# First projection of a hybrid decoder layer cut into quarters, with its convolution moved behind the second projection

## The chip, the cores and the metric

The kernel runs on one core of one Trainium2 chip. The metric is the device time of one execution in microseconds (us). Five engines of the core work from queues of their own, each in program order: PE (TensorE, the matmuls), DVE (VectorE), ACT (ScalarE), POOL (GpSimd) and SP (SyncE, which issues most of the transfers). Waits between them are semaphores.

## The reference, cut to what matters

One decoder layer for 256 tokens of width 1024: a mixer with four branches, a layer norm, a mixture of 16 experts, a layer norm. The change touches only the beginning of branch B (gated DeltaNet):

```python
proj = jnp.einsum("bsd,de->bse", x, w_in)          # x: 256 x 1024, w_in: 1024 x 10264
qkv = jax.nn.silu(causal_depthwise_conv(gdn_qkv, gdn_conv_w))   # gdn_qkv: 1536 columns of proj
q, k, v = jnp.split(qkv, [512, 1024], axis=-1)
```

## The kernel before

**Precision.** Every float32 operand of a projection is split in two parts that TensorE multiplies fast: a high part (a cast by ACT) and the rest (a subtraction by DVE, float32 minus high part). A product of two such operands is three matmuls: high by high, high by low, low by high. `split` does this for the transposed input (`xh`, `xl`), `parts` for a piece of weight (`whi`, `wlo`).

**Projections.** `w_in` is taken in pieces of 256 columns (1 MB). `fetch` loads a piece into one of three buffers `raw`, which it takes in turn. `proj_cm` casts a piece in two blocks of 128 columns (`parts`, three buffers each for `whi` and `wlo`) and multiplies each block by the whole of x: 24 matmuls of 256 columns for a block, 48 for a projection, into a PSUM tile `pcm` of pool `pmm`. This pool has three buffers, so the fourth projection waits until all readers of the first projection's tile are done, the fifth until those of the second are, and so on.

**The beginning.** Four transfers on SP bring x in halves (256 KB each), then come the first piece of weight in two halves, the second piece whole, thirteen small transfers (`prm_r`, `hp8`: parameters), and then the third piece and what follows. PE transposes x in groups of four 128x128 blocks (L264); ACT and DVE split each group (L101, L102). A projection's step `b_in(ci)` multiplies and then runs the causal convolution: per block one ACT scaling (L407) and three DVE multiply-adds (L410) that read the projection's PSUM tile. Its taps come from `taps()` (L336 to L340): PE transposes the parameters, DVE copies them out and scales them.

**What sets the order.** The text ORDER lists the steps. Inside that, a scheduler orders the instructions of PE, DVE, ACT and POOL; SP's are left in the order of the code. The steps at the start are `bi.0 cc bi.1 bi.2 cq.0 bi.3`: projections 1, 2 and 3 for branch B with their convolutions (`cc` computes constants in many tiny DVE operations), the fourth projection `cq.0` for branch C, the fifth for B again. All transfers share eight completion semaphores in rotation, and a transfer that takes a semaphore waits at its issue until the transfer eight places before it has landed.

Of the kernel before, what the change touches and what calls it, by code (L numbers as in the profile page):

```python
# [8 lines left out]
F32 = mybir.dt.float32  # L9
# [32 lines left out]
bi.0 cc bi.1 bi.2 cq.0 bi.3 sm bi.4 cq.1 bi.5 bs gg.0 bp.0 ll bv.0 cq.2 bp.1 bo lg.0  # L42
# [10 lines left out]
def trunk(ctx: ExitStack, tc: tile.TileContext, a, out):  # L53
# [45 lines left out]
    def split(ps, hi, lo, scale=None):  # L99
        if scale is None:  # L100
            A.copy(hi, ps)  # L101
            V.tensor_tensor(lo, ps, hi.bitcast(F32), op=OP.subtract)  # L102
# [7 lines left out]
    def fetch(src, cuts=1):  # L110
# [4 lines left out]
        for c in range(cuts):  # L115
            cs = slice(c * n // cuts, (c + 1) * n // cuts)
            Q.dma_start(raw[:, :, cs], src[:, :, cs])
        return raw

    def parts(raw, k0, nk, c0, n, one=None):  # L120
# [6 lines left out]
        cuts = (slice(0, nk),) if one is None else (slice(0, nk // 2), slice(nk // 2, nk))  # L127
        for c in cuts:
            if one is None:
                A.copy(hi, src)  # L130
            else:
                A.activation(hi[:, c], src[:, c], AF.Copy, scale=one)  # L132
        for c in cuts:
            V.tensor_tensor(lo[:, c], src[:, c], hi[:, c].bitcast(F32), op=OP.subtract)  # L134
# [68 lines left out]

    ones = mk.tile([128, 128], F32, name="ones")
    G.memset(ones, 1.0)
    one = cst.tile([128, 1], BF16, name="one")
# [52 lines left out]
    one0 = cst.tile([128, 1], F32, name="one0")  # L259
    for kg in range(2):  # L260
        for n in range(2):
            p = pb("pxt")
            for k in range(4):
                T.transpose(p[:, k, :], x0[n][:, (4 * kg + k) * 128:(4 * kg + k + 1) * 128], ident)  # L264
            split(p, xh[:, 4 * kg:4 * kg + 4, n * 128:(n + 1) * 128],
                  xl[:, 4 * kg:4 * kg + 4, n * 128:(n + 1) * 128])
    A.activation(one0, xh[:, 4, 0:1].bitcast(F32), AF.Copy, scale=0.0, bias=1.0)
# [1187 lines left out]
```

## Time and profile before

| | us |
|---|---|
| runs of the kernel before: median (lowest, highest) | 612.0 (611.89, 613.32) |
| the profiled execution, device time | 614.47 |
| its span, first to last instruction | 612.7 |
| PE busy in the span | 586.7 |
| DVE busy | 323.9 |
| ACT busy | 253.1 |

The profile is one execution. Times in its rows count from the start of the span. A row of the timeline gives start, duration, engine, line, operation, what it writes and reads, shape and count; in brackets stands how long the engine was idle before and what released it. When one instruction had several waits the profile names only one releaser, and it can name the wrong one: the program's order tells which instruction a wait is on.

### The profile page before, as it was taken

To read this page: it belongs to the slowest core of one execution; us is meant where nothing else is said; L and a number is where in the kernel's file an instruction comes from. 1 tells how busy PE (TensorE), PEld (TensorE's weight loads), DVE (VectorE), ACT (ScalarE), POOL (GpSimd) and SP (SyncE) were. 2 spreads that over 40 slices of the span, in tenths; PEclk is the share of its full clock that TensorE was granted. 3 is DMA by queue.
4 is the path that set the end of the run, shared out by engine and by line. 5 is a ranking of instruction groups with operands and counts; after the bars stand their busy time and mean duration, and the time that the engine had idled before them with its cause. 6 is when DMAs were issued, how large, how long until landed. Compare 5 with 4: busy or idle time off the path is not lost. (4 is left out here: it accounts for less than half of the span.)

```text
span 612.7 us, 10555 instructions
## 1 busy us (share of the span) xinstructions
PE 586.7 (96%) x4231; PEld 458.9 (75%) x4231; DVE 323.9 (53%) x651; ACT 253.1 (41%) x413; POOL 20.2 (3%) x53
## 2 busy tenths in 40 slices
PE   6999999999999999999999999999999999999992
PEld 5999999989988999999999999633633634444351
DVE  3799788678458955865656655552210300111245
ACT  5556664473478747644444444311201211021121
POOL 3000010100102000000000000000000000000000
PEclk9999999999999999999999999999999999999996
DMA  7877454632221564398998794789999999999931
GB/s 208 227 226 200 138 153 137 210 107 85 86 70 34 174 208 138 118 329 319 387 357 306 262 406 193 291 333 403 418 415 408 415 416 409 416 416 407 417 160 72
DMA packets 86380, 160.43 MB, mean 262 GB/s; under 512 B 9963, under 2 KB 56161, under 8 KB 86326
## 3 DMA queue, kind: packets, MB, share of 16 engines
q1 hardware_dynamic: 86198, 159.44, 71.6%
q8 instruction: 35, 0.57, 0.4%
q0 software_dynamic: 128, 0.26, 0.2%
q14 instruction: 19, 0.16, 0.1%
HBM read 158.50 MB, written 1.18 MB: 261 GB/s over the span
## 5 line engine op out<-in xcount | busy, mean ns | idle before, releaser
L134 DVE TENSOR_TENSOR wlo<-raw,whi 128x1024 fp32r<-128x1024 f32 (+1 forms) x106 | 126.0, 1200 | 53.7 <-ACT whi L130 53.0
L130 ACT CAST whi<-raw 128x1024 fp32r<-128x1024 f32 x102 | 106.1, 1047 | 97.6 <-DMA raw<-in_w_in_dram 33.0
L272 PE MATMUL pcm<-xh,whi 128*128 128x256 f32 x512 | 125.9, 284 | 1.9 <-ACT whi L132 1.5
L276 PE MATMUL pcm<-xl,whi 128*128 128x256 f32 x512 | 125.0, 282 | 0.0
L272 PEld LDWEIGHTS pcm<-xh,whi 128*128 128x128 f32 x512 | 97.2, 190 | 2.7 <-ACT whi L132 1.9
L276 PEld LDWEIGHTS pcm<-xl,whi 128*128 128x128 f32 x512 | 97.3, 190 | 0.1
L281 PE MATMUL pcm<-xh,wlo 128*128 128x256 f32 x512 | 71.6, 281 | 1.3 <-DVE wlo L134 1.1
L281 PEld LDWEIGHTS pcm<-xh,wlo 128*128 128x128 f32 x512 | 65.4, 189 | 1.7 <-DVE wlo L134 1.7
L102 DVE TENSOR_TENSOR dd<-pd,dd 128x512 fp32r<-128x512 f32 (+1 forms) x18 | 11.4, 632 | 95.3 <-ACT dd L101 95.3
L1303 PE MATMUL pd<-ew,sh 128*64 128x512 f32 (+1 forms) x288 | 56.8, 546 | 0.7 <-ACT sh L1364 0.7
L1292 PE MATMUL wu<-ew,xg 128*64 128x512 f32 x256 | 57.4, 593 | 0.0
L1292 PE MATMUL wg<-ew,xg 128*64 128x512 f32 x256 | 56.7, 595 | 0.6 <-issue 0.6
L1303 PEld LDWEIGHTS pd<-ew,sh 128*64 128x64 f32 x288 | 20.4, 137 | 35.1 <-issue 29.4
L1292 PEld LDWEIGHTS wu<-ew,xg 128*64 128x64 f32 x256 | 18.5, 137 | 36.2 <-issue 34.4
L1292 PEld LDWEIGHTS wg<-ew,xg 128*64 128x64 f32 x256 | 18.1, 137 | 33.5 <-issue 32.1
L272 PE MATMUL ptm<-whi,xh 128*128 128x256 f32 x128 | 32.5, 287 | 0.0
L272 PE MATMUL pbr<-yth,whi 128*128 128x256 f32 x128 | 32.1, 284 | 0.0
L276 PE MATMUL pbr<-ytl,whi 128*128 128x256 f32 x128 | 32.0, 282 | 0.0
L274 PE MATMUL ptm<-whi,xl 128*128 128x256 f32 x128 | 31.5, 281 | 0.0
L101 ACT CAST dd<-pd 128x512 fp32r<-128x512 f32 (+1 forms) x18 | 9.7, 538 | 46.3 <-PE pd L1303 46.3
L1209 ACT ACTIVATE xg<-pxg,gbp 128x128 f32<-128x128 f32 x32 | 13.2, 456 | 36.7 <-DVE xg L1208 35.7
L1343 DVE SCALAR_TENSOR_TENSOR sh<-wu,cw,sh 128x512 f32<-128x512 f32 x8 | 6.0, 750 | 37.9 <-PE wu L1292 37.8
(420 smaller groups left out, 887.4 us busy)
## 6 DMA issues: line engine op xcount, KB each, us to landing
raw<-in_w_in_dram SPq DMA_DIRECT2D x39, 1024.0 KB, 5.3
ew<-in_w_gate_dram SPq DMA_DIRECT2D x64, 512.0 KB, 9.8
ew<-in_w_up_dram SPq DMA_DIRECT2D x64, 512.0 KB, 9.7
ew<-in_w_down_dram SPq DMA_DIRECT2D x64, 512.0 KB, 9.8
raw<-in_w_branch_dram SPq DMA_DIRECT2D x8, 1024.0 KB
raw<-in_w_out_dram SPq DMA_DIRECT2D x4, 1024.0 KB
x<-in_x_dram SPq DMA_DIRECT2D x4, 256.0 KB, 5.3
raw<-in_w_in_dram SPq DMA_DIRECT2D x2, 512.0 KB
```

What stands on the lines that cost most here:

```text
L101: A.copy(hi, ps)
L102: V.tensor_tensor(lo, ps, hi.bitcast(F32), op=OP.subtract)
L130: A.copy(hi, src)
L134: V.tensor_tensor(lo[:, c], src[:, c], hi[:, c].bitcast(F32), op=OP.subtract)
L272: T.matmul(o, sh(k), mh(k), start=first and k == 0, stop=False)
L274: T.matmul(o, sl(k), mh(k), start=False, stop=False)
L276: T.matmul(o, sh(k), ml(k), start=False, stop=False)
L281: T.matmul(o, sl(k), mh(k), start=False, stop=last and k == kt - 1)
L1209: A.activation(xg[1][:, 2 * kg + k, :], ps[kg][:, k, 128:256], AF.Identity, scale=g_, bias=b_)
L1292: P(T.matmul(p[r, :], xg[pr][:, k, r], W[pr, (nm, e, k // 2)][:, k % 2, :], start=k == 0, stop=k == 7))
L1303: P(T.matmul(p[r, :], hT[:, k, r], W[pr, ("wd", e, k)][:, 0, c0:c1], start=k == 0, stop=k == 3))
L1343: V.scalar_tensor_tensor(sg, pu, cw[pr // 2][:, pr % 2:pr % 2 + 1], sg, op0=OP.mult, op1=OP.mult)
```

## The change

- x comes in quarters of 256 columns (eight transfers of 128 KB on SP), and the first piece of weight in four transfers of 256 KB, each with two of its eight row blocks and all 256 columns, issued by ACT instead of SP, one for each quarter of x. The third piece of weight is fetched in the code of the beginning too, behind the small parameters.
- `first_proj` replaces `proj_cm` for the first projection. It goes by quarters: transposes, split and casts of the next quarter stand in front of this quarter's 12 matmuls, and one PSUM accumulation runs over both blocks. In front of it, and between the first two transposes, stand 14 and 8 matmuls on a tile of zeros (`warm`), whose result is not used.
- The weight parts of the second projection are made at the end of `first_proj`. `b_in(0)` stops after its products; `b_in(1)` runs `taps()`, then the first convolution, then its own. In ORDER, `bi.1` stands ahead of `cc`.
- Several instructions are kept in the order of the code (`keep`, `K`). A constant 1.0 that was computed from xh (`one0`) is a memset (`one1`) now.

```diff
-bi.0 cc bi.1 bi.2 cq.0 bi.3 sm bi.4 cq.1 bi.5 bs gg.0 bp.0 ll bv.0 cq.2 bp.1 bo lg.0
+bi.0 bi.1 cc bi.2 cq.0 bi.3 sm bi.4 cq.1 bi.5 bs gg.0 bp.0 ll bv.0 cq.2 bp.1 bo lg.0
...
-    for h in range(2):
+    w0 = w_in[:, :, C_GQ:C_GQ + 256]
+    raw0 = [fetch(w0, 0)]
+    for q in range(4):
+        cs = slice(256 * q, 256 * q + 256)
         for n in range(2):
-            Q.dma_start(x0[n][:, 512 * h:512 * h + 512], xin[:, n, 512 * h:512 * h + 512])
-    raw0 = [fetch(w_in[:, :, C_GQ + 256 * j:C_GQ + 256 * j + 256], 2 - j) for j in range(2)]
+            Q.dma_start(x0[n][:, cs], xin[:, n, cs])
+        A.dma_start(raw0[0][:, 2 * q:2 * q + 2], w0[:, 2 * q:2 * q + 2])
+    raw0.append(fetch(w_in[:, :, C_GQ + 256:C_GQ + 512]))
...
+    raw0.append(fetch(w_in[:, :, C_GQ + 512:C_GQ + 768]))
...
+    def first_proj():
+        p = pmm.tile([128, 2, S], F32, name="pcm", tag="mm")
...
+        warm(14)
+        x_part(0)
+        w_part(0)
+        warm(8)
+        for q in range(4):
+            if q < 3:
+                x_part(q + 1)
+                w_part(q + 1)
+            hi = hl[q // 2][0][:, 2 * (q % 2):2 * (q % 2) + 2]
+            for k in range(2 * q, 2 * q + 2):
+                for b in range(2):
+                    for x in (xh, xl):
+                        K(T.matmul(p[:, b, :], hi[:, k % 2, 128 * b:128 * b + 128], x[:, k, :],
+                                   start=q == 0 and k == 0 and b == 0 and x is xh, stop=False))
+            low(q)
+        v.hl1 = [parts(raw0[1], 0, 8, 128 * b, 128, K) for b in range(2)]
+        return p
...
-        p = proj_cm(C_GQ + 256 * ci, raw0[ci] if ci < 2 else None, one0 if ci == 0 else None)
+        p = first_proj() if ci == 0 else proj_cm(C_GQ + 256 * ci, raw0[ci] if ci < 3 else None,
+                                                  v.hl1 if ci == 1 else None)
         if ci == 0:
+            v.first = p
+            return
+        if ci == 1:
             taps()
+            conv(0, c4, v.first)
+        conv(ci, c4, p)
```

The built programs show where the scheduler puts this. First DVE, around the first convolution. Before, it reads the first projection's tile (`pcm_216`) between the low parts of the third piece of weight (`raw_396`) and the first of the fourth (`raw_467`); the rows begin in its second block, and `splq` are tiny operations of `cc`:

```order
L134 TENSOR_TENSOR wlo_400<-raw_396,whi_399 128x1024
L410 SCALAR_TENSOR_TENSOR gq_215<-pcm_216,cwh_206,gq_215 128x255
L327 TENSOR_SCALAR splq_299<-splq_299 128x4
L134 TENSOR_TENSOR wlo_428<-raw_396,whi_427 128x1024
L410 SCALAR_TENSOR_TENSOR gq_215<-pcm_216,cwh_206,gq_215 128x254
L326 TENSOR_TENSOR splq_299<-splq_299,spls2_298 128x4
L134 TENSOR_TENSOR wlo_471<-raw_467,whi_470 128x1024
L410 SCALAR_TENSOR_TENSOR gq_215<-pcm_216,cwh_206,gq_215 128x253
L327 TENSOR_SCALAR splq_299<-splq_299 128x4
L410 SCALAR_TENSOR_TENSOR gq_215<-pcm_327,cwh_206,gq_215 128x255
```

The last reader of `pcm_216` stands just behind the first low part of the fourth piece, and the taps stand ahead of all these rows. Now, in the same place, with the third piece as `raw_145`, the fourth as `raw_498`, and the tiles of the first and second projection as `pcm_199` and `pcm_318`:

```order
L129 TENSOR_TENSOR wlo_459<-raw_145,whi_458 128x1024
L129 TENSOR_TENSOR wlo_502<-raw_498,whi_501 128x1024
L387 COPY prm_133<-pp_367 128x128
L388 TENSOR_SCALAR cwh_189<-prm_133 128x48
L395 TENSOR_SCALAR hb_190<-prm_133 128x4
L396 TENSOR_SCALAR hb_190<-prm_133 128x4
L398 TENSOR_SCALAR nlam_395<-prm_133 128x4
L466 SCALAR_TENSOR_TENSOR gq_198<-pcm_199,cwh_189,gq_198 128x255
L466 SCALAR_TENSOR_TENSOR gq_198<-pcm_318,cwh_189,gq_198 128x255
```

The taps (`prm`, `cwh`) have moved behind the first low part of the fourth piece, and the first convolution behind them. Six multiply-adds on block 0 of both tiles in turn begin here; DVE then goes on like this:

```order
L368 TENSOR_SCALAR spls_398<-sple_397 128x4
L129 TENSOR_TENSOR wlo_530<-raw_498,whi_529 128x1024
L466 SCALAR_TENSOR_TENSOR gq_198<-pcm_199,cwh_189,gq_198 128x255
L466 SCALAR_TENSOR_TENSOR gq_198<-pcm_318,cwh_189,gq_198 128x255
L466 SCALAR_TENSOR_TENSOR gq_198<-pcm_199,cwh_189,gq_198 128x254
L466 SCALAR_TENSOR_TENSOR gq_198<-pcm_318,cwh_189,gq_198 128x254
L466 SCALAR_TENSOR_TENSOR gq_198<-pcm_199,cwh_189,gq_198 128x253
L466 SCALAR_TENSOR_TENSOR gq_198<-pcm_318,cwh_189,gq_198 128x253
```

So the last reader of the first projection's tile (`pcm_199`, 128x253) has moved behind both low parts of the fourth piece, with five operations on the second projection's tile in front of it. The first instruction of PE's fourth projection waits on this one (and on ACT) in both programs, since it writes the same PSUM buffer; the fifth projection's waits on the last reader of the second projection's tile, the row below.

Then ACT, at the beginning of its queue. Before:

```order
L101 ACT_TABLE_LOAD
L101 CAST xh_174<-pxt_177 128x4x128 [waits PE_49]
L101 CAST xh_174<-pxt_184 128x4x128 [waits PE_49]
L101 CAST xh_174<-pxt_191 128x4x128 [waits PE_49]
L101 CAST xh_174<-pxt_198 128x4x128 [waits PE_49]
L267 ACTIVATE one0_176<-xh_174 128x1 [waits Activation_49]
L132 ACTIVATE whi_217<-raw_109,one0_176 128x512 [waits DMAHW4_49,Activation_49]
```

Now, with the transfers of the first piece of weight in front:

```order
L145 DMA raw_105<-in_w_in_dram 128x2x256 x3
L145 DMA raw_105<-in_w_in_dram 128x2x256 [waits DMAHW0_49]
L103 ACT_TABLE_LOAD
L103 CAST xh_184<-pxt_214 128x512 [waits PE_49]
L296 CAST whi_221<-raw_105 128x512
L103 CAST xh_184<-pxt_233 128x512 [waits PE_49]
L296 CAST whi_221<-raw_105 128x512 [waits DMAHW3_49]
```

The table load has moved behind four transfers, of which the fourth waits until the first has landed (`DMAHW0_49`).

On SP the row behind the eight quarters of x is the second piece of weight, then the thirteen small transfers, then the third and fourth pieces, as before. From the fifth projection on PE's rows are the same in both programs, and soon after the other engines' are too.

## Rows read from the trace of the kernel before

**Rows 1.** The profile's page, its parts 1 and 2: busy time by engine with its share of the span, and PE's busy tenths in 40 equal slices of the span.

```profile
PE 586.7 (96%) x4231; PEld 458.9 (75%) x4231; DVE 323.9 (53%) x651; ACT 253.1 (41%) x413; POOL 20.2 (3%) x53
PE   6999999999999999999999999999999999999992
```

**Rows 2.** Waits of PE in the whole span: line that waited, for whom, us in total, times, longest.

```profile
PE pn L1416 <- DVE nmc L1412: 5.9, 1, 5.9
...
PE p L570 <- DVE ps L565: 1.7, 2, 0.9
...
PE pcm L272 <- DVE splq L327: 0.4, 1, 0.4
```

**Rows 3.** Stretches of the span: start and end, us, busy us and instructions of PE, its weight loads, DVE, ACT and POOL, then the granted TensorE clock, the share of the DMA engines and GB/s.

```profile
10.20:15.26 5.06, 5.06 (x25) 5.06 (x25) 2.80 (x5) 3.18 (x5) 0.00 (x0) 1.00 0.48 151
...
30.00:60.00 30.00, 29.57 (x250) 29.11 (x249) 28.30 (x76) 18.79 (x30) 0.00 (x0) 1.00 0.77 222
```

**Rows 4.** Timeline of PE: the first transposes of x, the first products of projections 1, 3, 4 and 5, and in front of the fifth the last eight products of the fourth.

```profile
3.60 2.11 PE L264 MATMUL pxt<-ident,x 128*128 128x128 f32 x8 [3.60 <-POOL tri L209]
...
10.20 0.58 PE L272 MATMUL pcm<-xh,whi 128*128 128x256 f32 x1 [1.53 <-ACT whi L132]
...
23.85 0.28 PE L272 MATMUL pcm<-xh,whi 128*128 128x256 f32 x1
...
29.50 0.28 PE L272 MATMUL pcm<-xh,whi 128*128 128x256 f32 x1
...
34.22 1.10 PE L281 MATMUL pcm<-xh,wlo 128*128 128x256 f32 x8
35.70 0.36 PE L272 MATMUL pcm<-xh,whi 128*128 128x256 f32 x1 [0.38 <-DVE splq L327]
```

**Rows 5.** Timeline of SP's issues: the first small transfer that stood until the second piece had landed, the issue of the third, fourth and fifth pieces (one row), and the transfer behind them.

```profile
13.97 0.25 SPq L166 DMA_DIRECT2D prm_r<-in_rg_b_x_dram  x1
...
16.16 2.84 SPq L117 DMA_DIRECT2D raw<-in_w_in_dram  x3
19.05 2.75 SPq L380 DMA_DIRECT2D raws<-in_w_in_dram  x1
```

**Rows 6.** Timeline of ACT: its table load and first cast of x, the casts of the second piece, the first convolution's scaling, and the first casts of the third and fourth pieces, which stood until those had landed.

```profile
0.80 1.28 ACT L101 ACT_TABLE_LOAD   x1 [0.80 <-PEq L1443]
4.73 0.58 ACT L101 CAST xh<-pxt 128x512 fp32r<-128x512 f32 x1 [2.65 <-PE pxt L264]
...
13.97 2.00 ACT L130 CAST whi<-raw 128x1024 fp32r<-128x1024 f32 x2 [1.56 <-DMA raw<-in_w_in_dram]
...
19.00 0.47 ACT L407 ACTIVATE gq<-pcm,cwh 128x256 f32<-128x256 f32 x1 [0.97 <-DVE cwh L340]
...
21.68 1.05 ACT L130 CAST whi<-raw 128x1024 fp32r<-128x1024 f32 x1 [1.88 <-DMA raw<-in_w_in_dram]
...
26.10 1.05 ACT L130 CAST whi<-raw 128x1024 fp32r<-128x1024 f32 x1 [2.06 <-DMA raw<-in_w_in_dram]
```

**Rows 7.** Timeline of DVE: the copy of the taps, the first multiply-add of a convolution, a low part of weight and the last multiply-add on the first projection's tile behind it, and later multiply-adds in a stretch without idle time.

```profile
18.40 0.29 DVE L339 COPY prm<-pp 128x128 f32<-128x128 f32 x1 [0.16 <-PE pp L338]
...
19.51 0.48 DVE L410 SCALAR_TENSOR_TENSOR gq<-pcm,cwh,gq 128x255 f32<-128x255 f32 x1 [0.39 <-ACT gq L407]
...
27.18 1.23 DVE L134 TENSOR_TENSOR wlo<-raw,whi 128x1024 fp32r<-128x1024 f32 x1 [1.13 <-ACT whi L130]
28.32 0.47 DVE L410 SCALAR_TENSOR_TENSOR gq<-pcm,cwh,gq 128x253 f32<-128x253 f32 x1
...
33.24 0.47 DVE L410 SCALAR_TENSOR_TENSOR gq<-pcm,cwh,gq 128x255 f32<-128x255 f32 x1
33.63 0.16 DVE L327 TENSOR_SCALAR splq<-splq 128x4 f32<-128x4 f32 x1
33.70 0.47 DVE L410 SCALAR_TENSOR_TENSOR gk<-pcm,cwh,gk 128x255 f32<-128x255 f32 x1
...
35.09 0.47 DVE L410 SCALAR_TENSOR_TENSOR gq<-pcm,cwh,gq 128x253 f32<-128x253 f32 x1
```

**Rows 8.** Timeline of PE at the end of the span: the last product before its longest idle time, and the next instruction.

```profile
598.50 0.28 PE L1313 MATMUL py<-dd,ST 128*128 128x256 f32 x1
604.64 0.58 PE L1416 MATMUL pn<-ident,nmc 128*5 128x128 f32 x2 [5.86 <-DVE nmc L1412]
```

**Rows 9.** Stretches with the columns of rows 3, of which the granted clock (third from the right) is read: the step between mixer and experts, and the idle time of rows 8.

```profile
380.20:383.60 3.40, 3.29 (x15) 3.29 (x16) 3.02 (x24) 3.36 (x6) 0.00 (x0) 0.50 1.03 402
...
384.00:386.00 2.00, 1.75 (x18) 1.63 (x16) 0.19 (x1) 0.58 (x1) 0.00 (x0) 1.00 1.02 389
...
598.80:602.00 3.20, 0.00 (x0) 0.00 (x0) 3.20 (x10) 1.09 (x1) 0.00 (x0) 1.00 0.03 8
602.00:604.60 2.60, 0.00 (x0) 0.00 (x0) 1.41 (x9) 0.29 (x1) 0.00 (x0) 0.51 0.04 9
```

**Rows 10.** Stretches of one us with the same columns; the last number, GB/s, is read.

```profile
2.00:3.00 1.00, 0.00 (x0) 0.00 (x0) 0.00 (x0) 0.08 (x1) 1.00 (x9) 1.00 0.82 285
...
8.00:9.00 1.00, 0.66 (x4) 0.26 (x2) 0.69 (x1) 0.47 (x2) 0.00 (x0) 1.00 1.18 296
...
11.00:12.00 1.00, 1.00 (x6) 1.00 (x6) 0.64 (x2) 0.92 (x2) 0.00 (x0) 1.00 1.08 343
12.00:13.00 1.00, 1.00 (x7) 1.00 (x6) 1.00 (x2) 0.42 (x1) 0.00 (x0) 1.00 0.43 129
```

More of the change, by code (lines that the diff above doesn't have):

```diff
@@ L108, in trunk, with fetch @@
     w_in = a["w_in"][0].rearrange("(k p) c -> p k c", p=128)
-    def fetch(src, cuts=1):
+    def fetch(src, rows=None):
         k, n = src.shape[1], src.shape[2]
@@ L114, in fetch, with parts @@
         raw = raw.rearrange("p (k c) -> p k c", k=k)
-        for c in range(cuts):
-            cs = slice(c * n // cuts, (c + 1) * n // cuts)
-            Q.dma_start(raw[:, :, cs], src[:, :, cs])
+        if rows is None:
+            Q.dma_start(raw, src)
         return raw
-    def parts(raw, k0, nk, c0, n, one=None):
+    def parts(raw, k0, nk, c0, n, keep=lambda i: i):
         hi = wst.tile([128, 1024], F32R, name="whi", tag="whi", bufs=NHI)[:, :nk * n]
@@ L126, in parts @@
         src = raw[:, k0:k0 + nk, c0:c0 + n]
[L127 to L134, printed above, removed]
+        keep(A.copy(hi, src))
+        keep(V.tensor_tensor(lo, src, hi.bitcast(F32), op=OP.subtract))
         return hi, lo
@@ L258, in trunk @@
     xl = xtp.tile([128, 8, S], F32R, name="xl")
-    one0 = cst.tile([128, 1], F32, name="one0")
-    for kg in range(2):
-        for n in range(2):
[L262 to L267, printed above, removed]
+    wz = mk.tile([128, S], BF16, name="wz")
@@ new lines, in trunk, with warm, x_part, low @@
+    V.memset(wz, 0.0)
+    idle = pb("idle", (128, S))
+    def warm(n):
+        for _ in range(n):
+            K(T.matmul(idle, wz[:, 0:128], wz, start=True, stop=True))
+    def x_part(q):
+        ps = pb("pxt", (128, 2, S))
+        for n in range(2):
+            for k in range(2):
+                K(T.transpose(ps[:, k, n * 128:(n + 1) * 128], x0[n][:, (2 * q + k) * 128:(2 * q + k + 1) * 128], ident))
+        split(ps, xh[:, 2 * q:2 * q + 2, :], xl[:, 2 * q:2 * q + 2, :], keep=K)
+    def first_proj():
+        p = pmm.tile([128, 2, S], F32, name="pcm", tag="mm")
+        hl = {}
+        def low(q):
+            for k in range(2 * q, 2 * q + 2):
+                for b in range(2):
+                    K(T.matmul(p[:, b, :], hl[q // 2][1][:, k % 4, 128 * b:128 * b + 128], xh[:, k, :],
+                               start=False, stop=k == 7 and b == 1))
+        def w_part(q):
+            if q % 2 == 0:
+                hl[q // 2] = [wst.tile([128, 1024], F32R, name=nm, tag=nm, bufs=NHI).rearrange("p (k c) -> p k c", k=4)
+                              for nm in ("whi", "wlo")]
+            raw = raw0[0][:, 2 * q:2 * q + 2]
+            hi, lo = (t[:, 2 * (q % 2):2 * (q % 2) + 2] for t in hl[q // 2])
+            K(A.copy(hi, raw))
+            K(V.tensor_tensor(lo, raw, hi.bitcast(F32), op=OP.subtract))
+        warm(14)
[7 more added lines that the diff above has]
+            hi = hl[q // 2][0][:, 2 * (q % 2):2 * (q % 2) + 2]
+            for k in range(2 * q, 2 * q + 2):
+                for b in range(2):
+                    for x in (xh, xl):
[4 more added lines that the diff above has]
+        return p
@@ L281, in mm3, with proj_cm @@
                 T.matmul(o, sl(k), mh(k), start=False, stop=last and k == kt - 1)
-    def proj_cm(c0, raw=None, one=None):
+    def proj_cm(c0, raw=None, hl=None):
         if raw is None:
@@ L288, in proj_cm @@
         for b in range(2):
-            hi, lo = parts(raw, 0, 8, 128 * b, 128, one)
+            hi, lo = hl[b] if hl else parts(raw, 0, 8, 128 * b, 128)
             mm3(p[:, b, :], lambda k: hi[:, k, :], lambda k: lo[:, k, :],
@@ L337, in taps @@
         pp = pb("pp", (128, 128))
[L338 removed]
+        K(T.transpose(pp, prm_r, ident))
         V.tensor_copy(prm, pp)
```

17 lines of the change are left out of this document (10 added, 7 removed).

## The prediction

> **What bounds the kernel now.** I read the busy times first: PE works 586.7 of 612.7 us, and in the 40 slices only the first and the last are not full [rows 1]. So the kernel is as long as PE's queue plus PE's idle time, and the list of PE's waits says where that is: 5.9 us near the end, and otherwise small pieces such as 1.7 and 0.4 us [rows 2]. A microsecond saved or lost at the start thus shifts all that follows, unless PE waits later for something that did not shift. The loads after the start do shift, since a buffer is free only when PE and DVE have used it.
>
> Then I read the start. PE transposes from 3.60 and multiplies from 10.20 [rows 4]. Its first 25 products take 5.06 us, 0.20 each [rows 3]; from 23.85 to 29.50 the third projection's 48 take 5.65 us, 0.118 each [rows 4]. So the first products run at the lower of TensorE's two levels (1.2 GHz), the later ones at 2.4, though the column of the granted clock reads 1.00 in both places. From 15.3 on PE has no gap up to 35.2. There the fourth projection's last eight products (34.22, at 0.118 each) are through, and the fifth starts at 35.70, 0.5 us late [rows 4]. The profile names a tiny `splq` as releaser; by the program it is the release of the second projection's PSUM tile: its last multiply-add starts on DVE at 35.09, takes 0.47, and PE starts 0.14 after its end [rows 7]. DVE has 28.30 us of work in the 30 us from 30.00 on [rows 3]. The loads leave no room either: ACT stood until 21.68 for the third piece of weight and until 26.10 for the fourth [rows 6]. So around 30 us PE, DVE and the loads are all close to their limits, and the question for this change is which of them comes last when the fourth projection wants to start, at 29.50 before.
>
> **The first projection.** It should end earlier. The 22 products on zeros (0.20 each, 4.5 us) stand in time in which PE was idle, up to 3.60 and between the groups of transposes. On ACT the table load (1.28 us, done at 2.08 before [rows 6]) now waits behind a transfer that needs the first one landed. The first quarter of x and of the weight are 0.5 MB; at 285 GB/s from 2.0 [rows 10] they are moved by 3.9, so with half a us for the landing and half for the issue the load starts near 4.9 and the first cast of x near 6.2, 1.5 us after the 4.73 of before. Cast of x, cast of weight and rest of x (three operations of 0.6 to 0.7) then let PE multiply from 7.5. A quarter is 12 products (1.4 us), and four transposes cost 0.5 (eight took 2.11 at the low level [rows 4], half of that at the high one); the chain of ACT and DVE for a quarter is about 2 us and runs beside them. 7.5 plus 4 x 1.4 plus 2 x 0.55 gives 14.2, where before the second projection started at 18.1. That is the saving that the change can have: up to 3.9 us. I assume that PE is at the high level by then, since it works from 1.2 us on almost without a gap.
>
> **The loads.** Do the next pieces come earlier too? The second piece landed at 13.97 [rows 5]. Up to then 3.1 MB are moved, before and now. The first piece's halves, in rows of 512 B, moved at 296 GB/s, the second piece, in rows of 1 KB, at 343 [rows 10]. Now all rows have 1 KB: the first piece takes 3.1 instead of 3.5 us, and x, which moved no faster than 285, gains up to 0.6. I take 0.9 in all, landing at 13.0; bounds are 12.3 and 14.5, the late end if the eight quarters of x, which wait for semaphores of each other, leave gaps. The Trainium skill, DMA: Bandwidth & Descriptors, section "Issuing engines are not separate DMA queues", speaks against the part on ACT: transfers of both engines share the same 16 DMA engines, and a second issuer saves issue time alone. No row before has a load from ACT; by this rule with no gain in rate the landing stays at 13.97 and the forecast below becomes 619.4.
>
> Behind the second piece nothing has moved on SP: the small transfers stand until it has landed, six issues follow, and then the third piece, 2.2 us later (13.97 to 16.16 [rows 5]). It landed 5.5 us after that and the fourth 9.9 us after it (16.16 to 26.10 [rows 5, 6]). So the third piece lands at 20.7 and the fourth at 25.1, wherever its `fetch` stands in the code: what PE wins at the first projection, the loads don't follow.
>
> **The wait that comes last.** PE's third projection needs the third piece's cast (1.05 us), so it runs from about 21.9 to 27.5. The fourth projection writes the first projection's PSUM buffer, whose last reader has moved. I count from the landing of the fourth piece, since DVE's queue is in order and the low part of this piece stands ahead of the taps:
> - cast on ACT, and 1.08 later (26.10, 27.18 [rows 6, 7]) the low part on DVE, 1.14 to the next (27.18 to 28.32): 2.2;
> - copy of the taps to the first scaling on ACT 0.6 (18.40 to 19.00), from there to the first multiply-add 0.5 (19.51): 3.3;
> - six multiply-adds on block 0 of both tiles, 0.39 each and a tiny one at 0.07 (33.24, 33.63, 33.70 [rows 7]), 2.5: 5.8;
> - the low part of the fourth piece's second block, 1.14: 6.95;
> - five multiply-adds on block 1 in turn; the second waits for its scaling, which stands behind a cast on ACT, and starts at 7.35. The fifth, the last on the first tile, starts at 8.55 and ends at 9.03;
> - PE 0.14 later: 9.2.
>
> So the fourth projection starts at 25.1 + 9.2 = 34.3, where it was 29.50: **4.8 us late**, after PE stood still from 27.5, 6.8 us. Nothing on PE can fill that time, its queue is in order. The fifth projection's wait of 0.5 us falls away, since its tile is read 0.4 us later than this one. That is +4.3, and the saving of the first projection lies wholly inside the idle time.
>
> **The clock.** After its longest idle time of before (last product at 598.50, next at 604.64 [rows 8]) PE was granted 1.00 up to 602.00 and 0.51 from there on [rows 9]. That idle time, 5.9 us, is shorter than the 6.8 us here, so I count on a fall here too. How long the low level lasts after that: from 10.20 it was 5 us [rows 3], at 380.20 3.4 us, with 1.00 in the stretch from 384.00 [rows 9]. In 5.06 us PE made 25 products, worth 2.9 us at the high level: 2.1 us lost; in 3.4 us 1.4. It may be none, if the clock stays, and 3.1, if it comes back half as much later again as at 10.20. I take 2.1, since the row at 10.20 is also one of a start in the middle of a projection.
>
> **Sum.** Behind the fourth projection PE has the same queue as before, with loads and DVE at least as far ahead as they were, and full slices to the end; 4.8 - 0.5 + 2.1 = +6.4. The profiled span of 612.7 becomes 619.1; the median of the runs, 612.0, becomes **618.4 us**.
>
> **Rivals.**
> (1) The idle time is as long, but the clock stays up or comes back soon: +4.3 to +5.0, about 616.5. Against it stands the idle time of rows 8, with its fall.
> (2) The loads come later than before, because four transfers of ACT and waiting quarters of x mix: landing at 14.5, +5.8, and the late clock, together 620.9.
> (3) The change does what its words say and is faster. Then the convolutions are out of the way when PE comes: PE starts the second projection at 14.2 and runs on, -3.8, 608.2. It decides at the landing of the fourth piece: for a fourth projection no later than 29.50 it must be there by 20.3, 5.8 us ahead of before, and for the whole saving by 16.5. The chain on SP allows that only if the second piece landed at 8.2; 3.1 MB at 343 GB/s from 2.0 need until 11. I see nothing for it but that a rate of landing can surprise.
> (4) The first projection does not gain, because the products on zeros don't raise the clock or ACT's table load comes late. At 0.20 its 48 products end near 18. This changes nothing: the wait at the fourth projection hangs on the loads and DVE, and the time is again 618.4.
>
> **Chances.** The forecast, with (4) inside it, has 0.70; (1) 0.12; (2) 0.10; (3) 0.05; a landing so early that loss and saving meet, 0.03. About 0.3% (1.8 us) is what a measurement of this kernel can tell from no change. Faster by more than that: 0.05; within it: 0.03; slower: 0.92. The range reaches from +2.5 (early landing, 3.6, with an operation less in the count and the clock staying up) to +9 (rival 2): 614.5 to 621.0, which leaves out rival (3) and little else.
>
> **What would show it.** In the profile of the changed kernel PE's row in front of the fourth projection should have about 7 us idle, released by DVE (a multiply-add of the convolution or the tiny operation behind it), and the granted clock should fall to 0.50 there and come back before 45. ACT's casts of the third and fourth piece should start near 20.7 and 25.1, SP's issue of them near 15.2. The second projection should start near 14.5. If the idle time is there but shorter than 4 us, the count on DVE is wrong; if it isn't there at all, the reading of the PSUM buffers is. If the end is late by more than the shift at 45 us, something behind has changed that I took as equal.

## The result, and the profile after

The changed kernel is slower: 620.15 us median (617.96 to 620.8, 4 runs) against 612.66 us of the kernel before on the same chip (611.89 to 613.78, 4 runs); the ratio is 1.0113 with a 95% interval of 1.0096 to 1.013. The forecast was 618.4, with 0.92 for slower. The profiled execution took 619.76 us with a span of 617.5, against 614.47 and 612.7 before.

The page, parts 1 and 2, PE's row and its row of slices [rows 1]:

```profile
PE 590.3 (96%) x4253; PEld 461.8 (75%) x4253; DVE 324.3 (53%) x653; ACT 252.4 (41%) x412; POOL 20.2 (3%) x53
...
PE   9789999999999999999999999999999999999992
```

PE's span grew by 4.8 us, its busy time by 3.6. The busy time contains the 22 products on zeros and the stretches at the low clock. The new idle time is in the second and third slices (15.4 to 46.3 us). The list of PE's waits in the whole span names it; the last wait of before that stood at the start was 0.4 us for a `splq` [rows 2], and 5.9 at the end is unchanged:

```profile
PE pn L1472 <- DVE nmc L1468: 5.9, 1, 5.9
PE pcm L320 <- DVE gq L466: 3.5, 1, 3.5
PE pcm L320 <- ACT whi L128: 2.5, 1, 2.5
```

The timeline of PE shows the two new waits in place: the first products of projections 1 to 5 (before they began at 10.20, 18.1, 23.85, 29.50, 35.70 [rows 4]):

```profile
7.29 0.39 PE L311 MATMUL pcm<-xh,whi 128*128 128x256 f32 x1
...
14.15 0.28 PE L320 MATMUL pcm<-xh,whi 128*128 128x256 f32 x1
...
22.56 0.38 PE L320 MATMUL pcm<-xh,whi 128*128 128x256 f32 x1 [2.48 <-ACT whi L128]
...
33.46 0.36 PE L320 MATMUL pcm<-xh,whi 128*128 128x256 f32 x1 [3.50 <-DVE gq L466]
...
40.73 0.28 PE L320 MATMUL pcm<-xh,whi 128*128 128x256 f32 x1
```

So PE is 3.95 us ahead at the second projection, only 1.3 at the third, 4.0 behind at the fourth, 5.0 behind at the fifth. The fourth projection itself took 7.27 us, where the third of the kernel before took 5.65. Why the third and fourth came late is told by SP, ACT and DVE. The issues on SP [rows 5]: the second piece, the first small transfer that stood until it had landed, the third to fifth pieces, and the transfer behind them:

```profile
5.87 0.43 SPq L118 DMA_DIRECT2D raw<-in_w_in_dram  x1
...
12.25 0.25 SPq L165 DMA_DIRECT2D prm_r<-in_rg_b_x_dram  x1
...
14.43 4.15 SPq L118 DMA_DIRECT2D raw<-in_w_in_dram  x3
18.63 2.80 SPq L428 DMA_DIRECT2D raws<-in_w_in_dram  x1
```

ACT: the table load, the first cast of x, and the casts of the second, third and fourth pieces [rows 6]:

```profile
4.83 1.28 ACT L103 ACT_TABLE_LOAD   x1 [4.83 <-DMA raw<-in_w_in_dram]
6.13 0.59 ACT L103 CAST xh<-pxt 128x512 fp32r<-128x512 f32 x1
...
12.39 2.00 ACT L128 CAST whi<-raw 128x1024 fp32r<-128x1024 f32 x2
21.46 2.00 ACT L128 CAST whi<-raw 128x1024 fp32r<-128x1024 f32 x2 [7.07 <-DMA raw<-in_w_in_dram]
24.47 1.04 ACT L128 CAST whi<-raw 128x1024 fp32r<-128x1024 f32 x1 [1.01 <-DMA raw<-in_w_in_dram]
```

The second piece landed 1.7 us earlier than before, the third only 0.2, the fourth 1.6. DVE, from the low parts of the third piece to the last reader of the first projection's tile [rows 7]:

```profile
22.54 2.36 DVE L129 TENSOR_TENSOR wlo<-raw,whi 128x1024 fp32r<-128x1024 f32 x2 [6.70 <-ACT whi L128]
25.54 1.23 DVE L129 TENSOR_TENSOR wlo<-raw,whi 128x1024 fp32r<-128x1024 f32 x1 [0.64 <-ACT whi L128]
26.69 0.28 DVE L387 COPY prm<-pp 128x128 f32<-128x128 f32 x1
...
27.74 2.43 DVE L466 SCALAR_TENSOR_TENSOR gq<-pcm,cwh,gq 128x255 f32<-128x255 f32 x6 [0.33 <-ACT gq L463]
...
30.15 1.22 DVE L129 TENSOR_TENSOR wlo<-raw,whi 128x1024 fp32r<-128x1024 f32 x1
31.29 2.42 DVE L466 SCALAR_TENSOR_TENSOR gq<-pcm,cwh,gq 128x255 f32<-128x255 f32 x6
```

Here a reader should stop at 6.70. DVE did nothing from 15.84 to 22.54, and the convolution could have run there: both projections' tiles were finished before 20, and PE turned the taps at 19.81. But in DVE's queue the taps stand behind the low parts of the third piece and one of the fourth, and those wait for loads.

Stretches of the span (columns as in rows 3; the granted clock is the third from the right):

```profile
23.70:27.00 3.30, 3.30 (x18) 3.30 (x17) 2.63 (x4) 1.04 (x1) 0.00 (x0) 0.50 1.16 315
...
30.00:33.40 3.40, 0.00 (x0) 0.00 (x0) 3.40 (x9) 1.96 (x4) 0.00 (x0) 1.00 0.63 177
33.40:36.00 2.60, 2.54 (x13) 2.57 (x14) 2.60 (x9) 1.16 (x2) 0.00 (x0) 0.60 1.01 349
36.00:38.00 2.00, 2.00 (x13) 2.00 (x13) 1.57 (x4) 1.11 (x2) 0.00 (x0) 0.67 0.05 14
38.00:40.00 2.00, 2.00 (x19) 2.00 (x18) 1.76 (x4) 0.31 (x1) 0.00 (x0) 1.00 0.01 4
```

After each of the two idle stretches the granted clock falls to 0.50, the lower level (1.2 GHz): from about 23.7 to 27.0 inside the third projection, and from about 33.9 to 37.3 inside the fourth. From 30.0 to 33.4 PE is idle while DVE is full. Behind 45 nothing changed: PE is 4.95 us later at the first `psmall`, the product behind the fifth projection (46.38 against 41.43), and the span is 4.8 longer.

### The profile page after: what moved, and what is told of

Its sections match the earlier page's. It is cut to its first block, busy times and chain, and to the rows that moved or that the text cites. A ratio compares the mean times of both kernels' runs of the same rounds, so it can differ in the third digit from the quotient of the medians.

```text
span 617.5 us, 10605 instructions
## 1 busy us (share of the span) xinstructions
PE 590.3 (96%) x4253; PEld 461.8 (75%) x4253; DVE 324.3 (53%) x653; ACT 252.4 (41%) x412; POOL 20.2 (3%) x53
## 3 DMA queue, kind: packets, MB, share of 16 engines
q10 hardware_dynamic: 1088, 1.05, 0.5%
## 5 line engine op out<-in xcount | busy, mean ns | idle before, releaser
L129 DVE TENSOR_TENSOR wlo<-raw,whi 128x1024 fp32r<-128x1024 f32 x102 | 123.4, 1220 | 54.7 <-ACT whi L128 54.0
L320 PE MATMUL pcm<-xh,whi 128*128 128x256 f32 x496 | 122.0, 284 | 6.0 <-DVE gq L466 3.5
L324 PE MATMUL pcm<-xl,whi 128*128 128x256 f32 x496 | 121.4, 282 | 0.0
L320 PEld LDWEIGHTS pcm<-xh,whi 128*128 128x128 f32 x496 | 94.5, 191 | 6.6 <-issue 3.8
L324 PEld LDWEIGHTS pcm<-xl,whi 128*128 128x128 f32 x496 | 94.6, 191 | 0.1
L329 PE MATMUL pcm<-xh,wlo 128*128 128x256 f32 x496 | 69.9, 283 | 2.2 <-DVE wlo L129 2.1
L329 PEld LDWEIGHTS pcm<-xh,wlo 128*128 128x128 f32 x496 | 63.8, 191 | 2.8 <-DVE wlo L129 2.8
L1359 PEld LDWEIGHTS pd<-ew,sh 128*64 128x64 f32 x288 | 20.4, 137 | 35.1 <-issue 30.3
L1348 PEld LDWEIGHTS wg<-ew,xg 128*64 128x64 f32 x256 | 18.1, 137 | 33.5 <-issue 32.4
L322 PE MATMUL ptm<-whi,xl 128*128 128x256 f32 x128 | 31.4, 280 | 0.0
L103 ACT CAST dd<-pd 128x512 fp32r<-128x512 f32 (+1 forms) x18 | 9.7, 539 | 46.3 <-PE pd L1359 46.3
```

Of the source, the lines that this page charges most:

```text
L103: keep(A.copy(hi, ps))
L129: keep(V.tensor_tensor(lo, src, hi.bitcast(F32), op=OP.subtract))
L320: T.matmul(o, sh(k), mh(k), start=first and k == 0, stop=False)
L322: T.matmul(o, sl(k), mh(k), start=False, stop=False)
L324: T.matmul(o, sh(k), ml(k), start=False, stop=False)
L329: T.matmul(o, sl(k), mh(k), start=False, stop=last and k == kt - 1)
```

## The experiments

**Theory A (release).** The fourth projection waits for the last reader of the first projection's PSUM tile, which the move of the convolution put behind both low parts of the fourth piece; the idle time, and the low clock behind it, are the loss. **Theory B (loads).** The third piece comes no earlier, PE runs out of work at the third projection, and the loss comes from loads that the new start has disturbed.

**1. The first projection's tile gets a buffer of its own.** Nothing else of the change is undone.

```diff
-    pbr = psm.enter_context(tc.tile_pool(name="pbr", bufs=5, space=PSUM))
+    pbr = psm.enter_context(tc.tile_pool(name="pbr", bufs=4, space=PSUM))
...
-        p = pmm.tile([128, 2, S], F32, name="pcm", tag="mm")
+        p = pmm.tile([128, 2, S], F32, name="pcm", tag="mm1", bufs=1)
```

> The changed kernel, with a PSUM buffer of its own for the first projection (pbr has four buffers in place of five to make room). Theory A (the loss is the fourth projection's wait for the release of the first projection's PSUM tile, and the clock behind it): the order of DVE and the loads stay, but the fourth projection follows the third at about 29.9, the row of 3.5 us idle goes, so does the second fall of the clock, and 3.5 + 1.6 us come back: 615, within 1 us of 612.7 + 0 to 2. Theory B (the loss comes from the loads: PE stood 2.5 us for the third piece, and what follows is late by that): the third projection still starts at 22.6, and nothing comes back: 619 to 620.

612.16 us against 612.48; ratio 0.9991 (0.9978 to 1.0004). PE's waits in its timeline from 20 to 38 us:

```profile
21.54 0.38 PE L320 MATMUL pcm<-xh,whi 128*128 128x256 f32 x1 [1.28 <-ACT whi L128]
36.08 1.21 PE L329 MATMUL pcm<-xh,wlo 128*128 128x256 f32 x8 [1.12 <-DVE wlo L129]
```

The fourth projection follows the third without a gap and the clock stays at 1.00. The whole loss is gone, with the moved convolution and the order of the loads as they were: A holds, B falls. In this execution the third piece also came 1.0 us earlier (its cast starts at 20.44, not 21.46), which by itself could not give back 7.5 us. The saving of 3.9 us is not there either: 1.28 goes to the third piece, 1.12 to a low part on DVE. What the buffer taken from `pbr` costs by itself was not tried.

**2. The convolution back in its place, the quarters kept.**

```diff
-bi.0 bi.1 cc bi.2 cq.0 bi.3 sm
+bi.0 cc bi.1 bi.2 cq.0 bi.3 sm
...
-            v.first = p
-            return
-        if ci == 1:
             taps()
-            conv(0, c4, v.first)
```

> The changed kernel with the first convolution back in the step of the first projection (taps and convolution straight behind its products, cc ahead of the second projection); quarters, zeros and loads as changed. Theory A: DVE is through with the first projection's tile near 30.8, so PE stands about 1 us there instead of 3.5: 613.5 to 615.5. Theory B (loads): nothing comes back, 619 to 620.

613.91 against 612.48; 1.0015 (1.0000 to 1.0029): the loss of the move is away here too.

```profile
23.03 0.58 PE L320 MATMUL pcm<-xh,whi 128*128 128x256 f32 x1 [2.20 <-ACT whi L128]
30.55 0.36 PE L320 MATMUL pcm<-xh,whi 128*128 128x256 f32 x1 [0.16 <-DVE splq L374]
```

The quarters alone bring nothing: the third projection waits 2.20 for its piece and runs partly at the low clock, and the fourth starts 1.05 later than in the kernel before.

**3. The move alone, in the kernel before** (its halves, its loads, its first projection).

```diff
-bi.0 cc bi.1 bi.2 cq.0 bi.3 sm
+bi.0 bi.1 cc bi.2 cq.0 bi.3 sm
...
+            v.first = p
+            return
+        if ci == 1:
             taps()
+            conv(0, c4, v.first)
```

> The kernel before with the first convolution moved behind the second projection and nothing else (no quarters, no zeros, loads as before). Theory A: the move alone makes the loss. The fourth piece lands at 26.1, 9.0 us later PE gets the tile: fourth projection at 35.1 in place of 29.5, 5.6 late, less 0.5 for the vanished wait, plus 1.6 of clock: +6.7, 619.4. Theory B (the quarters and their loads make it): the move costs under 1 us, 612 to 613.5.

618.3 against 612.48; 1.0090 (1.0067 to 1.0113). In PE's timeline, and in ACT's the cast of the fourth piece:

```profile
34.06 0.54 PE L272 MATMUL pcm<-xh,whi 128*128 128x256 f32 x1 [5.01 <-DVE gq L417]
```

```profile
26.11 1.05 ACT L130 CAST whi<-raw 128x1024 fp32r<-128x1024 f32 x1 [2.21 <-DMA raw<-in_w_in_dram]
```

The move makes the loss by itself. From the cast to PE it is 7.95 us, against 9.0 in the changed kernel: the expectation (35.1, 5.6 late) took over the 9.0 of the changed kernel, but here DVE has the taps ahead of the fourth piece's first low part, and the count is that much shorter.

**4. The third piece issued ahead of the small transfers.**

```diff
     raw0.append(fetch(w_in[:, :, C_GQ + 256:C_GQ + 512]))
+    raw0.append(fetch(w_in[:, :, C_GQ + 512:C_GQ + 768]))
...
-    raw0.append(fetch(w_in[:, :, C_GQ + 512:C_GQ + 768]))
```

> The changed kernel with the third piece of weight issued ahead of the thirteen small transfers. Theory A: the third projection starts near 20 without a gap, and ends near 25.8, but the fourth still waits for the tile, which hangs on the landing of the fourth piece (about 23.2) plus 9.0: start near 32.2, idle 6.4, clock falls once: 616 to 617. Theory B (PE's wait for the third piece is the loss): that wait is gone, and so is the loss: 612.7 or less.

619.49 against 612.48; 1.0115 (1.0091 to 1.0138): no better than the changed kernel, and outside both expectations (616 to 617; 612.7 or less).

```profile
31.82 0.55 PE L319 MATMUL pcm<-xh,whi 128*128 128x256 f32 x1 [6.05 <-DVE gq L465]
```

The third projection starts at 20.0 without a gap, so the wait of 2.5 us is gone, and all of it is waited at the fourth instead. The fourth piece was cast at 22.82, 9.0 before PE, as in the changed kernel. B falls a second time. The start came 1.6 earlier, of which the low clock took back 0.4 (it lasted 6.8 us here, partly in the idle time): at the first `psmall` PE is 3.7 us late instead of 4.95. The medians don't show that difference.

**5 and 6. Cure both.** With the third piece early, experiment 5 fixes DVE's order by hand (low parts of the third piece, taps, first convolution, low parts of the fourth, second convolution), and experiment 6 adds the buffer of experiment 1. The edit of 5, beside that of 4:

```diff
+            v.hl1 = [parts(raw0[2], 0, 8, 128 * b, 128, K) for b in range(2)]
...
-            conv(0, c4, v.first)
-        conv(ci, c4, p)
+            conv(0, c4, v.first, K)
+            v.raw4 = fetch(w_in[:, :, C_SQ:C_SQ + 256])
+            v.hl4 = [parts(v.raw4, 0, 8, 128 * b, 128, K) for b in range(2)]
+        conv(ci, c4, p, K if ci == 1 else lambda i: i)
```

> The changed kernel with the third piece issued ahead of the small transfers, and an order fixed for ACT and DVE: parts of the third piece, taps, first convolution, parts of the fourth piece, second convolution. The theory of the release says that with the first convolution done by about 24 and the fourth piece there by 23, the fourth projection starts near 25.8 without a wait, and nearly the whole saving of the first projection (4 us) reaches the end: 608 to 610. A rival says that a new wait takes its place (the fifth projection, which takes over the buffer of the fourth, or DVE as the bound), and the time stays within 1.5 us of the kernel before: 611 to 614.

> The changed kernel with the third piece issued ahead of the small transfers and a PSUM buffer of its own for the first projection (pbr four buffers); order as changed. The theory of the release: the fourth projection follows the third at 25.6; the fifth waits until 32.2 for the second convolution, and then for a low part, so 2.5 to 3.5 us of the saving reach the end: 609 to 610. The rival (DVE is the bound whatever PE waits for): no better than with the tile alone, 612.

Experiment 5: 612.04 against 612.92, 0.9981 (0.9965 to 0.9997). Experiment 6: 611.79, 0.9983 (0.9969 to 0.9997). Both are a little faster, by no more than just clear of the noise, and short of what the theory of the release expected of them (608 to 610; 609 to 610); the times are those of the rivals (611 to 614; 612). In 5 the fourth and the fifth projection wait:

```profile
26.85 0.39 PE L319 MATMUL pcm<-xh,whi 128*128 128x256 f32 x1 [0.78 <-ACT whi L128]
33.45 0.39 PE L319 MATMUL pcm<-xh,whi 128*128 128x256 f32 x1 [0.68 <-ACT sq L739]
```

In 6 the fifth waits 0.71 at 32.27, and 1.12 at 35.51 for a low part. With the early waits cured, other ones come last. In 6 these are the second projection's tile and a low part. In 5 the built program puts the fifth projection's tile into the buffer of the fourth, not of the second, so it waits for ACT's copy of the fourth (`sq`).

**7. Without the 22 products on zeros,** whose result is not used (`warm` and its tile are left out).

> The changed kernel without the 22 products on zeros. The prediction's rival (4): the first projection then runs at 0.20 a product from its start and ends near 17 to 18 instead of 14.15, but the wait at the fourth projection hangs on the loads and DVE alone, so the time stays: 619 to 620.5. If the zeros matter for what follows (clock in the third and fourth projection), it differs by more than 1 us.

617.53 against 612.92; 1.0097 (1.0069 to 1.0125). PE's timeline:

```profile
7.62 0.58 PE L300 MATMUL pcm<-xh,whi 128*128 128x256 f32 x1
...
10.59 0.36 PE L300 MATMUL pcm<-xh,whi 128*128 128x256 f32 x1
...
15.49 0.28 PE L309 MATMUL pcm<-xh,whi 128*128 128x256 f32 x1
...
33.82 0.43 PE L309 MATMUL pcm<-xh,whi 128*128 128x256 f32 x1 [4.98 <-DVE gq L455]
```

Only the first quarter's products ran at the low level (0.21 each), so the first projection ended at 15.5 and not at 17 to 18. The zeros are worth 1.3 us there and nothing at the end, as rival (4) had it. The time is even lower than the 619 to 620.5 that were expected, but the intervals of the two ratios overlap, and the runs scatter from 616.99 to 621.22. In its profile PE waits 1.51 us for the third piece instead of 2.48, and the granted clock stays at 1.00 there and near 380 us; three of the four runs have a mean granted clock of 0.986 to 0.988, where the changed kernel has 0.981 to 0.984. Whether leaving out the zeros brings that about is not shown.

**8. The kernel before once more,** unaltered, for the scatter.

> The kernel before, once more. The profile of before shows a fall of the clock near 380 us of 3.4 us, which other profiles do not have. If that fall is the difference between its 614.5 and the median of 612.5, a second profile is either near 612.5 us without the fall, or near 614.5 with it; if it has nothing to do with it, the time and the fall go separate ways.

612.15 us; ratio 0.9995 (0.9982 to 1.0008). Its profiled execution took 614.12 us and has the fall near 380 again. That fits the fall as the cause of the 614.5, but does not settle it, for there is a second fall here; and other profiles do have the one near 380, that of the changed kernel among them. The second fall is inside the third projection, behind a wait; PE's row, and a stretch with the columns of rows 3:

```profile
23.56 0.38 PE L272 MATMUL pcm<-xh,whi 128*128 128x256 f32 x1 [1.93 <-ACT whi L130]
```

```profile
25.00:28.30 3.30, 3.30 (x19) 3.30 (x18) 3.30 (x8) 2.35 (x3) 0.00 (x0) 0.51 0.82 167
```

In this execution the first projection ran at 0.118 a product, and the second started at 15.74, 2.4 us ahead of rows 4's execution. But the third piece was cast only at 22.46 (21.68 there), so PE stood for it, and at the first `psmall` it is 0.7 us behind (42.15 against 41.43). The kernel before, unaltered, shows what the prediction said of the loads: what PE wins at the first projection, they don't follow.

**9. The convolution as early as can be:** in the step of the first projection, with the third piece issued by ACT in the middle of it.

```diff
+            if q == 2:
+                w2 = w_in[:, :, C_GQ + 512:C_GQ + 768]
+                raw0.append(fetch(w2, 0))
+                K(A.dma_start(raw0[2], w2))
...
-            v.first = p
-            return
+            conv(0, c4, p, K)
+            v.hl2 = [parts(raw0[2], 0, 8, 128 * b, 128, K) for b in range(2)]
+            return
```

> The changed kernel with the first convolution at its earliest place: taps and first convolution straight behind the first projection's products, ACT and DVE held to the order first convolution, parts of the third piece, second convolution; the third piece of weight issued by ACT in the middle of the first projection instead of by SP behind the small transfers. Theory (the saving is there if neither the tile's release nor the third piece is late): the first projection's tile is free near 19.5, the third piece lands near 16 to 17, third projection near 20.3, fourth near 26, fifth near 31.7, 4 us ahead of before: 608 to 610. Rival (DVE is the bound in the first 40 us, as in the run that put both in order): 611 to 612.

614.5 against 612.0; 1.0044 (1.0023 to 1.0065), slower than both the theory (608 to 610) and the rival (611 to 612) expected. ACT's timeline, then PE's:

```profile
12.64 0.37 ACTq L299 DMA_DIRECT2D raw<-in_w_in_dram  x1
13.06 0.59 ACT L103 CAST xh<-pxt 128x512 fp32r<-128x512 f32 x1 [2.10 <-DMA prm_r<-in_conv_a_b_dram]
```

```profile
14.21 0.39 PE L313 MATMUL pcm<-xh,whi 128*128 128x256 f32 x1 [1.13 <-ACT whi L294]
17.70 0.30 PE L388 MATMUL pp<-ident,prm_r 128*128 128x128 f32 x1 [1.72 <-DMA hp<-in_gdn_a_log_dram]
```

The issue stood on ACT 2.10 us for a small transfer whose semaphore it shares, the cast of the fourth quarter stood behind it, and PE's queue waited for the parameters at 17.70. A wait in an engine's queue had been moved from the fourth projection to the first.

**10. The first piece's quarters issued by SP** instead of ACT.

```diff
-        A.dma_start(raw0[0][:, 2 * q:2 * q + 2], w0[:, 2 * q:2 * q + 2])
+        Q.dma_start(raw0[0][:, 2 * q:2 * q + 2], w0[:, 2 * q:2 * q + 2])
```

> The changed kernel with the four transfers of the first piece of weight issued by SP, each behind its quarter of x, instead of by ACT. If the second issuer made the second piece land 1.7 us earlier than before (12.25 against 13.97), it lands now between 13.2 and 14.5, and the third and fourth pieces and the fourth projection move back by as much: 620.5 to 622. If it was the size of the rows, it lands at 12.3 again and the time stays 619 to 620.5.

619.44 against 612.0; 1.0111 (1.0085 to 1.0137): as the changed kernel. SP's issue of the second piece, and of the small transfer that stands until it has landed:

```profile
6.89 0.47 SPq L118 DMA_DIRECT2D raw<-in_w_in_dram  x1
...
14.47 0.25 SPq L165 DMA_DIRECT2D prm_r<-in_rg_b_x_dram  x1
```

The second piece is issued 1.0 later than in the changed kernel and lands 2.2 later. The last number of these two stretches, first of the changed kernel and then of this one, is the GB/s that the DMA engines moved:

```profile
4.00:11.00 7.00, 7.00 (x49) 6.04 (x48) 3.42 (x6) 4.60 (x7) 1.70 (x10) 1.00 1.08 373
```

```profile
4.00:11.00 7.00, 6.14 (x53) 5.62 (x52) 3.96 (x6) 3.47 (x7) 1.71 (x10) 1.00 0.98 294
```

The kernel before moved 302 in the same stretch. So the size of the rows by itself is not what made the second piece early: here they are 1 KB too, and it lands at 14.47, as the first alternative had it, though the time is that of the second. The third and fourth pieces are cast at 23.00 and 26.01, 1.5 later, but the fourth projection starts at 34.30, only 0.84 later: from the cast to PE it is 8.3 us.

**11. Both cures and a fourth buffer for all projections.** As 5, with `pmm` at four buffers (`pbr` gives one up), the last operations of the first convolution behind the fourth piece's low parts, and `cc` behind `sm`.

```diff
-    pmm = psm.enter_context(tc.tile_pool(name="pmm", bufs=3, space=PSUM))
-    pbr = psm.enter_context(tc.tile_pool(name="pbr", bufs=5, space=PSUM))
+    pmm = psm.enter_context(tc.tile_pool(name="pmm", bufs=4, space=PSUM))
+    pbr = psm.enter_context(tc.tile_pool(name="pbr", bufs=4, space=PSUM))
...
-bi.0 bi.1 cc bi.2 cq.0 bi.3 sm
+bi.0 bi.1 bi.2 cq.0 bi.3 sm cc
...
+            tail(0, c4, K)
```

> The third piece is issued ahead of the small transfers, the matmul PSUM pool gets a fourth buffer (the broadcast pool gives one up), and the order of the Vector engine's work is fixed by hand: third piece's low parts, taps, first convolution, fourth piece's low parts, second convolution. The squared copy in front of the fifth projection is no longer in its way. If the releases of PSUM buffers and not the amount of the Vector engine's work decide, the fourth projection starts at about 25.8 us, the fifth at about 31.5, and the time is 609 to 610.5 us. If the Vector engine's own work between 20 and 42 us is the bound by now, the fifth projection waits for it again, and the time is 611.5 to 612, as with the two versions before.

609.2 us (608.42 to 611.4, 6 runs) against 612.45; ratio 0.9949 (0.9930 to 0.9968): faster than both kernels. Stretches, columns as above, and from DVE's timeline the last reader of the first projection's tile:

```profile
20.00:25.00 5.00, 5.00 (x44) 5.00 (x43) 4.28 (x20) 2.99 (x7) 0.00 (x0) 1.00 1.09 362
25.00:30.00 5.00, 5.00 (x45) 5.00 (x44) 5.00 (x9) 3.93 (x7) 0.00 (x0) 1.00 1.00 244
30.00:35.00 5.00, 5.00 (x44) 5.00 (x44) 4.74 (x9) 3.24 (x7) 0.00 (x0) 1.00 0.70 228
```

```profile
24.44 0.48 DVE L470 SCALAR_TENSOR_TENSOR gq<-pcm,cwh,gq 128x253 f32<-128x253 f32 x1
```

PE has no gap and the clock no fall there, nor near 380. With four buffers the fifth projection, which now starts at 31.4, takes over the first projection's, whose last reader is the one at 24.44; in 5 it stood until ACT had copied the fourth's tile. From 20 to 40 us DVE is as full as in 5 (18.96 us of work against 18.66), so the amount of its work is not the bound: in 5 PE waited for a cast and for that copy, both on ACT (0.78 and 0.68). How much of the gain over 5 is the buffer and how much the moved `cc` was not tried apart. At the first `psmall` PE is 4.4 us ahead of before; 3.0 are left from about 125 us on.

**12. The changed kernel once more,** unaltered.

> The changed kernel once more, unaltered, to size the loss from more executions. By the profiled executions (+4.8 us of span) the median would be about 617 to 618 us; by the medians of the first comparison (+7.5) it is 619 to 620.5. If the larger difference holds, the profile should again show the fall of the clock at the fourth projection, and the kernel before should again run below its own profiled time.

619.65 us (618.82 to 621.38) against 612.45; 1.0113 (1.0096 to 1.0131). The larger difference holds. Its profile has the wait again, and a longer stretch at the low level (to about 39.3, span 619.2):

```profile
33.37 0.55 PE L320 MATMUL pcm<-xh,whi 128*128 128x256 f32 x1 [3.59 <-DVE gq L466]
```

## Why the prediction was right, point by point

- **The bound.** Right: PE's queue and its idle time set the end, and a shift at 45 us (+4.95) is the shift at the end (+4.8).
- **First projection.** Right: products from 7.29 (said 7.5), the second projection at 14.15 (said 14.2), the table load at 4.83 (4.9). All of the saving was lost before the fourth projection, as said. The 3.95 us are counted against one execution of the kernel before; against that of experiment 8, whose second projection starts at 15.74, they are 1.6.
- **Landings.** The second piece was there by 12.25, not 13.0, and the third was issued at 14.43, not 15.2. That it came early was forecast for a reason that does not hold, and so by luck: the 0.9 us stood for rows of 1 KB, and experiment 10 has these rows, 294 GB/s against the 302 of before, and a landing at 14.47, later than the 13.97 of before. By the Trainium skill, DMA: Bandwidth & Descriptors, section "Issuing engines are not separate DMA queues", a second issuer saves issue time alone. The trace shows more in this case: 1.0 us at the issue, 2.2 at the landing, and 373 GB/s with ACT as second issuer. But experiment 10 also puts the quarters of x and of weight into another order on SP; which of the two makes the other 1.2 was not tried. The third piece came at 21.46, not 20.7: it took 7.0 us from its issue, where I had carried over 5.5 from one execution (in experiment 8 the kernel before took 6.95). The two errors cancel in part, and the fourth was cast at 24.47 (said 25.1), 10.0 after the issue.
- **The count on DVE.** Right: 9.0 from the fourth piece's cast to PE, said 9.2; 9.0 again in experiment 4. It is a count of this order alone: 7.95 and 8.3 in experiments 3 and 10.
- **The wait.** Right in its mechanism, shown by experiments 1 (own buffer, no loss) and 3 (the move alone, the loss); its size and split were off. The fourth projection started at 33.46, not 34.3, so 4.0 late and not 4.8. I had PE idle 6.8 us in front of it, and it was 3.5. Besides the earlier start, the third projection ended at 29.96 and not at 27.5: it started later (22.56 against 21.9), and the clock fell inside it, behind an idle time of 2.5. My own times left 2.0 us idle there (14.2 + 5.65 to 21.9), and I asked neither for that wait's size nor for a fall behind it. The third projection's lost time is hidden in the wait at the fourth.
- **The clock at the fourth projection.** It fell and was back by 38, and cost 7.27 - 5.65 = 1.6 us, where 2.1 was the term. The reason given for it fails: I leaned on an idle time of 6.8, longer than the 5.9 of rows 8, but 3.5 were enough, and 2.5 at the third projection. Of the two durations that I had, the 3.4 us of rows 9 was the one that applied (the row at 10.20 holds 24 products, not 25, the last one only begins at its end; that makes 0.1 us); in experiments 4 and 12 it was 6.8, so the range was right to hold both.
- **Sum.** In the profiled executions 4.0 - 0.55 + 1.6 = +5.0 at the fifth projection and +4.8 at the end, not +6.4. The medians differ by more, 7.5. That 618.4 lies so close to 620.15 is therefore partly luck: a step that was 1.6 us too large for the profiles was added to a median that lies below its profile. Part of the difference between the two steps can be read from the runs: of the 11 of the kernel before beside experiment 12, eight have a mean granted clock of 0.991 or 0.992 and take 611.22 to 612.75, and three have 0.989 and take 613.18 to 614.08. The profiled execution of before is one of the latter (0.989), with a fall near 380 us [rows 9]; its median run is not. The nine runs of the changed kernel all have 0.981 to 0.984, and both of its profiles have the fall near 380 too. So about 1.5 us of the 7.5 (the difference of the means of those eight and three) is that my base was a profile of before with that fall; the rest stays open. That the change makes the fall near 380 more frequent is likely by these clocks, but was not shown by a run that controls it.
- **The rivals.** (1) is out, since the clock fell. (2) is out: the loads came earlier. (3) did not come true, and by its own condition it could not, with the fourth piece at 24.47 and not at 20.3; but the condition was put too narrowly. Experiment 11 has the gain with a fourth projection at 25.7, with the third piece early and the convolution put ahead of the fourth piece's low parts, so that the release no longer hangs on that landing. (4) was right that it doesn't matter, and wrong on the size: 15.5, not 18.

## What to carry to other kernels

A tile in a rotating pool is released by its last reader, so work that is moved later on one engine moves a start on another, here three projections later, as the pool has three buffers: look for that start before counting the time saved, and read from the built program which buffer it takes (in experiment 5 it was another). Ahead of a reader in an in-order queue, name what waits for a load, since the release then hangs on that load. A saving at the head of a queue that hardly ever empties was kept here only when the next waits were cured together (the load, the order on DVE and the fourth buffer, with `cc` moved too): the load alone left the loss as it was, two of them made 0.2% against the kernel before, all together 0.5%.

## What the runs showed of the hardware that was not expected

- The granted clock fell to 0.50 behind idle times of PE of 1.93 us (the kernel before in experiment 8), 2.20 (experiment 2), 2.48, 3.50, 5.01 (experiment 3) and 6.05 (experiment 4). It did not behind 1.28 (experiment 1), 1.51 (experiment 7), 1.71 (experiment 10) and 1.72 (experiment 9). These are the cases seen, not a bound. The fall lasted about 3.4 us in most cases and 6.8 in two (experiments 4 and 12). The fourth projection lost 1.6 us to one of 3.4 us, and 2.7 in experiment 12 (8.4 instead of 5.65).
- By the mean granted clocks, a fall near 380 us comes and goes between executions of the same kernel, at about 1.5 us each. What decides it stays open.
- In experiment 9 a small transfer that SP had issued by 9.5 us, behind the 1 MB second piece, had landed only at 12.64, and ACT, whose own issue shares its semaphore, stood 2.10 us for it with its casts behind.
